# Smaller TensorE prices in a kernel's ordering layer

## The chip, the cores and the metric

The kernel runs on one core of a Trainium2 chip. The metric is the device time of one execution, in microseconds (us). Before the change three runs gave 1128.09, 1132.45 and 1138.17 us, median 1132.45.

## The reference

One inference step of a two-layer backbone for 128 context tokens and 256 latent tokens, model width 1024, all in float32. In a layer:

```
h   = LN(x) * (1 + scale_a) + shift_a            # shift, scale, gate = silu(cond) @ ada_w + ada_b
z   = h @ w_in                                   # 1024 x 2048, split in q, k, v, conv and gating parts
A   = attention(rms(q), rms(k), v)               # 8 q heads, 2 kv heads; latents also see 128 cached keys
B   = c_b * conv3(c_c * c_in)                    # depthwise, width 3
C   = u * (W_s LN(v) + b)                        # over chunks of 128 positions
x   = LN1(alpha * x + gate_a * concat(A, B, C) @ w_out)
h   = LN(x) * (1 + scale_f) + shift_f
x   = LN2(alpha * x + gate_f * FFN(h))
```

FFN is a dense SwiGLU of width 2816 in layer 0 and top-2 of 8 SwiGLU experts of width 1408 in layer 1. There the router's logits choose two experts for each token, and the weights of all eight are read. The outputs are both token streams and each layer's context keys and values.

## The kernel before, in words

**Tiles.** The 384 tokens are three tiles of 128 rows. A product that must keep float32 accuracy takes three matmuls in the fp32r type (`mm3`, L647): both operands are split into a high and a low part. Weights arrive in 1 MB loads into five `st` buffers (768 or 512 KB at the edges of a matrix); ScalarE casts the high part of half a load (`wh`), VectorE subtracts to get the low part (`wl`) (`split`, L630, and `split2`, L1144). 1 MB of weights in a full block of 128 rows feeds 12 matmuls of 512 columns. The modulation (`ada_group`, L731), the small block of 32 rows and the two half blocks of 64 rows (`pair`, L1552) use the raw float32 weights.

**Stages.** Modulation for layer 0, the mixers of layer 0 (`mixers`, L958: `w_in`, attention, convolution, gating, `w_out`), the dense FFN (L1101), the mixers of layer 1, routing (`route`, L1205: LN, transposes, router logits, ranks and lists for three tiles), then the experts (`moe`, L1706): a first full block with a fixed expert, four full blocks in the order of their loads, and a last full block that shares its weights with a small block of 32 rows. The two least loaded experts share one block in two halves of 64 rows. Its 18 steps are put between steps of the full blocks, evenly over the list from the place in `PLACES = (4, 7, 56)` on; this is the shared block in small steps. `scatter` (L1656) and `back` (L1647) add the expert rows to the tokens, and `close_main` (L1675) writes the result.

**The ordering layer.** `Net` calls no engine directly. Each operation goes to `Plan.record` (L285), which notes its operands and gives it a price in ns for each engine that may do it (`price`, L364). `flush` (L403) then plays the program through with one clock for each engine: an operation is ready when those it needs have ended, plus a latency from `LAT` (L349). Of the ready ones of an engine, `flush` takes one that starts within `SLACKS` (50 ns on PE, 60 on DVE) of the time when the engine is free, in the order in which they were recorded, and otherwise the one that starts first. Then the instructions are issued in the order found. Each engine works its list in that order, whatever the real times turn out to be. An operation recorded through `nc.any` may go to one of two engines, and `finish` (L522) picks the one that the planned clocks favour.

A load's price is its bytes at 375 bytes per ns, 2796 ns for 1 MB. Buffers are given out by `find` (L173): a tile may be placed ahead of earlier tiles of its tag only if places are left for all of those. `WINDOW` (380) limits how far the plan looks ahead.

**Filling matmuls.** Where the plan sees PE idle, `keep_warm` (L502) issues matmuls of the identity, whose result nobody reads. They are in the program, and are executed there whether PE is really idle or not. Their number is

```
WARM = (500, 430)
n = int((at - f - WARM[0]) / WARM[1])
```

with `f` the planned time at which PE is free and `at` the planned start of its next operation. A planned gap must so be at least 930 ns to get one, and each further 430 ns gives one more. They are issued at L515; all other planned instructions are issued at L498, or at L500 if they are the second or later matmul of a group.

**Prices of PE before (L376 to L386).** A transpose costs 62 ns if its operand is fp32r, else 109. The 32-row strips of raw float32 cost 0.4167 ns for each column plus 12. The 64-row halves of 512 columns cost half of 1.6667 ns for each column plus 1. An fp32r matmul costs 0.4453 ns for each column plus 4, and at least 112: this is 232 ns for 512 columns and 175 for 384. Other float32 matmuls cost 1.6667 (or 0.85 at half the rows) for each column plus 6, and at least 214.

Of the kernel before, what the change touches and what calls it, by code (L numbers as in the profile page):

```python
# [11 lines left out]
F32R = mybir.dt.float32r  # L12
# [235 lines left out]
class Plan:  # L248
# [115 lines left out]
    def price(self, eng, name, outs, ins, a, k):  # L364

        if name == "call":
            return 1000.0 if outs else 100.0
        if name == "dma_start" and eng != "SP":
            return 60.0
        if eng == "SP":  # L370
            v = outs[0] if outs else ins[0]
            return v.free() * v.cells.shape[0] * 4 * 32 / 375.0
        o = outs[0]
        n = o.free()
        ps_in = any(v.tile.psum for v in ins)
        if eng == "PE":  # L376
            if name == "transpose":
                return 62 if ins[0].dt == F32R else 109
            if o.cells.shape[0] == 1 and ins[0].dt != F32R:
                return n * 0.4167 + 12  # L380
            if o.cells.shape[0] == 2 and len(ins) > 1 and ins[1].dt == F32 and "tile_position" in k and n == 512:
                return n * 1.6667 * o.cells.shape[0] / 4 + 1
            if ins[0].dt == F32R:
                return max(112, n * 0.4453 + 4)
            half = o.cells.shape[0] == 2 or ins[0].cells.shape[0] == 2
            return max(214 if len(ins)>1 else 107, n * (0.85 if half else 1.6667) + 6)  # L386
        if eng == "ACT":
            c = 0.833 * max(n, max([v.free() for v in ins], default=0)) + (55 if ps_in else 90)
            return c + 93 * sum(isinstance(k.get(q), View) for q in ("bias", "scale", "accum_out"))
        if eng == "POOL":  # L390
            if k.get("op") == ALU.pow:
                return 160 * n + 300
            return 2.25 * n + (245 if name == "tensor_scalar" else 80)
        m = max([n] + [v.free() for v in ins])
        if name in ("tensor_copy", "tensor_scalar", "tensor_scalar_add", "tensor_scalar_mul", "tensor_single_scalar"):
            extra = 50 * sum(isinstance(v, View) for v in a[2:])
            return (1.04 if ps_in else 0.52) * m + 70 + extra
        if name == "memset":
            return 0.3 * m + 60
        return 1.04 * m + 70 + (60 if name == "scalar_tensor_tensor" and isinstance(a[2], View) else 0)  # L400
# [1644 lines left out]
```

## Time and profile before

| | |
|---|---|
| median of three runs | 1132.45 us (1128.09 to 1138.17) |
| the profiled execution | 1130.28 us |
| its span, first to last instruction | 1128.5 us |
| mean granted TensorE clock | 0.984 of full |
| PE busy | 1083.0 us (96%), 5256 matmuls |
| DVE busy | 737.1 us (65%) |
| ACT busy | 537.7 us (48%) |
| POOL busy | 123.8 us (11%) |
| moved by DMA | 282.11 MB, mean 250 GB/s |

PE is TensorE's matrix part, PEld its weight loads, DVE VectorE, ACT ScalarE, POOL GpSimd, SP SyncE, which issues the loads. Busy time of PE is the union of its matmuls' intervals, which overlap; the rate of a stream of matmuls is therefore read from starts, not from the duration of one. A float32 matmul that is not fp32r stands in the trace as two matmuls. A waiting time names the engine that ended it. "Issue" is a wait that the profile can't put down to anything.

### The profile page before, as it was taken

The numbers are of one execution on the slowest core, as the hardware profiler recorded it, in microseconds if no ns is written. First come the engines' busy times: TensorE is split into PE (matmuls) and PEld (weight loads), VectorE is DVE, ScalarE is ACT, GpSimd is POOL, SyncE is SP. The second block draws the span as 40 slices with busy tenths as digits, with TensorE's granted clock in tenths as the row PEclk, the third lists the DMA queues.
The fourth block names the chain that finished last, engine by engine and source line by source line (L and its number), as shares of the span: only waits on it lengthen the run. The fifth ranks groups of instructions, "written<-read, shape, count | busy, mean of one in ns | idle before, by whom it ended". The sixth has DMA issues, their size and how long they took to land. (4 is left out here: it accounts for less than half of the span.)

```text
span 1128.5 us, 14587 instructions
## 1 busy us (share of the span) xinstructions
PE 1083.0 (96%) x5256; PEld 771.3 (68%) x5256; DVE 737.1 (65%) x1296; ACT 537.7 (48%) x900; POOL 123.8 (11%) x141
## 2 busy tenths in 40 slices
PE   7999999999999999989999989999999999999995
PEld 4566568877777778857666777666767677676673
DVE  3475769543434444697657896856757677787965
ACT  3544556431323233254554336455656555576652
POOL 3440103100000000034100120000000000002201
PEclk8999999999999999999999979999999999999998
DMA  9877553564647474554367536899889999897541
GB/s 369 311 276 287 193 188 139 197 211 162 238 172 272 150 288 139 222 221 157 118 246 241 204 125 224 321 359 381 332 340 373 389 386 357 341 360 265 212 175 59
DMA packets 49295, 282.11 MB, mean 250 GB/s; under 512 B 6320, under 2 KB 8112, under 8 KB 21312
## 3 DMA queue, kind: packets, MB, share of 16 engines
q1 hardware_dynamic: 47104, 275.51, 64.8%
q0 software_dynamic: 1248, 4.02, 1.0%
q10 hardware_dynamic: 864, 1.57, 0.4%
q8 instruction: 43, 0.70, 0.3%
q14 instruction: 36, 0.29, 0.1%
HBM read 277.63 MB, written 3.46 MB: 249 GB/s over the span
## 5 line engine op out<-in xcount | busy, mean ns | idle before, releaser
L498 PE MATMUL bank<-q,q 128*128 128x512 f32 (+6 forms) x3679 | 875.8, 391 | 4.2 <-DVE q L498 2.4
L498 PEld LDWEIGHTS bank<-q,q 128*128 128x128 f32 (+2 forms) x3679 | 654.5, 189 | 203.9 <-issue 34.4
L498 DVE TENSOR_TENSOR q<-st,q 128x1024 fp32r<-128x1024 f32 (+1 forms) x324 | 373.7, 1184 | 118.6 <-ACT q L498 94.3
L498 ACT CAST q<-st 128x1024 fp32r<-128x1024 f32 (+1 forms) x324 | 318.7, 1018 | 231.0 <-PE bank L498 124.6
L498 DVE TENSOR_TENSOR q<-q,bank 128x512 f32<-128x512 f32 (+3 forms) x121 | 70.5, 592 | 114.9 <-PE bank L498 108.2
L498 ACT COPY q<-bank 128x128 f32<-128x128 f32 (+2 forms) x201 | 64.1, 370 | 88.6 <-PE bank L498 61.3
L498 PE MATMUL bank<-idf,q 128*128 128x128 f32 (+1 forms) x503 | 82.3, 287 | 24.1 <-ACT q L498 10.5
L498 PEld LDWEIGHTS bank<-idf,q 128*128 128x128 f32 (+1 forms) x503 | 59.4, 145 | 63.5 <-ACT q L498 18.8
L498 POOL TENSOR_TENSOR q<-q,nhalf 128x1 f32<-128x1 f32 (+3 forms) x42 | 41.5, 995 | 461.3 <-DVE q L498 461.3
L498 POOL TENSOR_TENSOR q<-q,q 128x512 fp32r<-128x512 f32 (+4 forms) x70 | 66.9, 972 | 220.7 <-ACT q L498 140.9
L498 ACT CAST q<-bank 128x512 fp32r<-128x512 f32 (+2 forms) x58 | 31.7, 554 | 110.4 <-PE bank L498 105.0
L498 PE MATMUL bank<-st,q 128*64 128x512 f32 (+3 forms) x280 | 84.1, 578 | 0.0
L498 DVE TENSOR_TENSOR q<-bank,q 128x512 fp32r<-128x512 f32 (+5 forms) x83 | 50.4, 616 | 44.5 <-ACT q L498 38.9
L500 PE MATMUL bank<-st,q 128*64 128x512 f32 (+1 forms) x140 | 64.2, 581 | 0.0
L498 DVE TENSOR_TENSOR q<-q,q 128x512 f32<-128x512 f32 (+13 forms) x135 | 54.5, 426 | 13.6 <-POOL q L498 10.7
L498 ACT ACTIVATE q<-bank 128x512 f32<-128x512 f32 (+4 forms) x51 | 26.2, 514 | 66.3 <-PE bank L498 57.9
L498 PE MATMUL bank<-st,cs 128*32 128x512 f32 x96 | 47.5, 609 | 1.1 <-DMA st<-in_ada_w_dram 0.8
L500 PE MATMUL bank<-st,cs 128*32 128x512 f32 x288 | 47.9, 609 | 0.0
L498 ACT ACTIVATE q<-bank,q 128x384 f32<-128x384 f32 (+2 forms) x58 | 30.9, 537 | 29.3 <-DVE q L498 22.8
L276 POOL DMA_INDIRECT q<-dr,q x8 | 9.4, 1169 | 313.9 <-DVE q L498 309.8
L498 PEld LDWEIGHTS bank<-st,q 128*64 128x64 f32 (+1 forms) x280 | 20.2, 122 | 33.9 <-issue 33.4
L498 DVE SCALAR_TENSOR_TENSOR q<-q,q,q 128x512 f32<-128x512 f32 (+2 forms) x45 | 41.0, 966 | 0.1
(87 smaller groups left out, 443.2 us busy)
## 6 DMA issues: line engine op xcount, KB each, us to landing
st<-in_ada_w_dram SPq DMA_DIRECT2D x48, 1024.0 KB
st<-in_moe_w2a_dram SPq DMA_DIRECT2D x40, 1024.0 KB
st<-in_moe_w1a_dram SPq DMA_DIRECT2D x32, 1024.0 KB
st<-in_moe_w3a_dram SPq DMA_DIRECT2D x32, 1024.0 KB
st<-in_ffn_w_dram SPq DMA_DIRECT2D x22, 1024.0 KB
st<-in_w_in_dram SPq DMA_DIRECT2D x16, 1024.0 KB
st<-in_moe_w1b_dram SPq DMA_DIRECT2D x16, 768.0 KB
st<-in_moe_w3b_dram SPq DMA_DIRECT2D x16, 768.0 KB
```

Of the source, the lines that this page charges most:

```text
L276: self.nc.gpsimd.indirect_dma_start(out=out, out_offset=None, in_=src.rearrange("p t d -> (p t) d"), in_offset=o)
L498: getattr(self.real[o.eng], o.name)(*a, **k)
L500: getattr(self.real[o.eng], o.name)(*[x.real() if isinstance(x, View) else x for x in b], **q)
```

## The change

Five constants of `price` for PE are replaced. Nothing else in the program is changed: not the operations, not the record order, not the places of the shared block's steps.

```
         if eng == "PE":
             if name == "transpose":
-                return 62 if ins[0].dt == F32R else 109
+                return 57 if ins[0].dt == F32R else 107
             if o.cells.shape[0] == 1 and ins[0].dt != F32R:
-                return n * 0.4167 + 12
+                return n * 0.4167 + 8
             if o.cells.shape[0] == 2 and len(ins) > 1 and ins[1].dt == F32 and "tile_position" in k and n == 512:
                 return n * 1.6667 * o.cells.shape[0] / 4 + 1
             if ins[0].dt == F32R:
-                return max(112, n * 0.4453 + 4)
+                return max(54, n * 0.4167 + 1 if n >= 256 else n * 1.6667 + 1)
             half = o.cells.shape[0] == 2 or ins[0].cells.shape[0] == 2
-            return max(214 if len(ins)>1 else 107, n * (0.85 if half else 1.6667) + 6)
+            return max(107, n * (0.85 if half else 1.6667) + 3)
```

So an fp32r matmul of 512 columns goes from 232 to 214 ns in the plan, one of 384 from 175 to 161, one of a few columns from 112 to 54; a router matmul (8 columns) and a small block's sum (32 columns) from 214 to 107; a transpose from 109 to 107.

## Rows read from the trace of the kernel before

**Rows 1.** Busy time by stage: window, length, engines' busy us, clock, DMA share, GB/s.

```profile
0.00:30.00 30.00, 23.92 (x110) 13.03 (x110) 10.18 (x30) 11.48 (x21) 9.56 (x24) 0.89 0.93 372
30.00:200.00 170.00, 166.78 (x905) 113.11 (x897) 117.71 (x261) 89.63 (x223) 41.68 (x45) 1.00 0.61 230
200.00:460.00 260.00, 258.97 (x1195) 202.76 (x1195) 113.49 (x138) 81.52 (x101) 2.67 (x3) 1.00 0.58 210
460.00:645.00 185.00, 176.88 (x890) 120.46 (x889) 139.99 (x298) 86.07 (x214) 35.01 (x42) 1.00 0.54 193
645.00:700.00 55.00, 48.56 (x228) 39.54 (x228) 45.12 (x133) 26.31 (x35) 9.68 (x10) 0.84 0.47 164
700.00:1100.00 400.00, 392.37 (x1886) 273.10 (x1886) 294.30 (x411) 235.23 (x296) 19.68 (x14) 1.00 0.85 327
1100.00:1128.00 28.00, 15.53 (x58) 9.26 (x54) 16.31 (x28) 7.46 (x13) 5.55 (x6) 0.84 0.16 59
```

**Rows 2.** Timeline of PE: a run of fp32r matmuls and what follows it.

```profile
639.71 7.37 PE L498 MATMUL bank<-q,q 128*128 128x512 f32 x31
646.91 1.55 PE L515 MATMUL bank<-idr 128*128 128x512 f32 x6
```

**Rows 3.** PE's costliest group, shapes apart: count, busy us, mean ns, idle before.

```profile
L498 PE MATMUL bank<-q,q 128*128 128x512 f32 x3036 | 757.4, 401 | 4.2 <-DVE q L498 2.4 <-ACT q L498 1.3
```

**Rows 4.** The filling matmuls' line: windows 0-30, 30-600, 600-700, 700-1128 us.

```profile
L515 PE MATMUL bank<-idr x29: 387/505/797, 1.7 to 23.9; 128*128 128x512 f32 x29
L515 PE MATMUL bank<-idr x4: 396/436/497, 499.5 to 503.2; 128*128 128x512 f32 x4
L515 PE MATMUL bank<-idr x33: 387/397/774, 646.9 to 675.6; 128*128 128x512 f32 x33
L515 PE MATMUL bank<-idr x2: 397/439/481, 901.3 to 951.0; 128*128 128x512 f32 x2
```

**Rows 5.** Timeline of PE in the routing: logits, filling matmuls, transposes.

```profile
651.55 3.54 PE L498 MATMUL bank<-q,q 128*128 128x8 f32 x16
654.94 2.05 PE L515 MATMUL bank<-idr 128*128 128x512 f32 x4
656.94 1.81 PE L498 MATMUL bank<-idf,q 128*128 128x128 f32 x8
658.73 1.95 PE L498 MATMUL bank<-q,q 128*128 128x8 f32 x16
...
673.43 2.52 PE L515 MATMUL bank<-idr 128*128 128x512 f32 x10
678.12 1.18 PE L498 MATMUL bank<-idf,q 128*128 128x128 f32 x8 [2.17 <-DMA q<-dr,q]
```

**Rows 6.** The page's DMA issues: the experts' loads.

```profile
st<-in_moe_w2a_dram SPq DMA_DIRECT2D x40, 1024.0 KB
st<-in_moe_w1a_dram SPq DMA_DIRECT2D x32, 1024.0 KB
st<-in_moe_w3a_dram SPq DMA_DIRECT2D x32, 1024.0 KB
...
st<-in_moe_w1b_dram SPq DMA_DIRECT2D x16, 768.0 KB
st<-in_moe_w3b_dram SPq DMA_DIRECT2D x16, 768.0 KB
...
st<-in_moe_w2b_dram SPq DMA_DIRECT2D x8, 512.0 KB
```

**Rows 7.** Waits of VectorE, experts' stage: who, for whom, us, times, longest.

```profile
DVE q L498 <- PE bank L498: 37.9, 22, 3.9
```

**Rows 8.** Busy time by stage, the 50 us with the busiest VectorE.

```profile
1000.00:1050.00 50.00, 48.87 (x238) 35.48 (x236) 41.99 (x46) 33.70 (x43) 11.21 (x8) 1.00 0.82 309
```

**Rows 9.** Waits of PE's weight loads for ACT and DVE, 460-645 us.

```profile
PEld bank L498 <- ACT q L498: 9.9, 19, 2.5
PEld bank L498 <- DVE q L498: 5.3, 11, 0.8
```

## The prediction

> **What bounds the kernel now.** I read the busy times by stage first [rows 1]. TensorE is the bound nearly everywhere: 258.97 of 260 us in the dense FFN, 392.37 of 400 in the experts, 176.88 of 185 in the second mixers, 166.78 of 170 in the first. All idle time of PE that a better order could remove is therefore small: 3.2 us in the first mixers, 8.1 in the second, 6.4 in the routing, 7.6 in the experts, 25.3 in all. The start (DMA share 0.93) and the tail after 1100 us, where the last LN runs out, hold the rest, and no price of PE changes what is late there.
>
> Then the rate of PE's main work. In a run of 31 fp32r matmuls, starts lie (646.91 - 639.71) / 31 = 232 ns apart [rows 2]. This is exactly the price before. The new price, 214 ns, is 17.7 ns or 7.6% short, and there are 3036 such matmuls [rows 3]: in the plan PE becomes some 54 us shorter, on the chip nothing does. The change removes no operation. It can act only through three things that the plan decides: the order on each engine, the engine of an `any` operation, and the number of filling matmuls.
>
> The Trainium skill (TensorE: Matmul & The Clock Gate, Back-to-back issue gap) gives N / 2.4 + 2.5 ns between matmuls at full clock, 216 for 512 columns, which is the new price. By that rule the new plan would run in step with the chip and the experts' term below would be nothing instead of 2 us. The trace disagrees, with its 232 ns [rows 2], and the measurement decides.
>
> **Part by part.**
>
> *Dense FFN, 200 to 460 us.* PE has 1.0 us idle in 260 [rows 1], the loads take 0.58 of the DMA's time and DVE less than half. Weights are split ahead, up to the buffers. Whatever the order, PE's sum remains: 0 us. The cover is PE's own saturation; it goes only if DVE's list were reordered so that splits came late, and DVE has 146 us free.
>
> *Filling matmuls.* Before there are 29 in the start, 4 at the change of layers, 33 in the routing, 2 in the experts [rows 4]. Each is a real instruction of some 0.23 us at full clock, as any of 512 columns [rows 2]. A cheaper PE is idle longer in the plan, so their number grows.
>
> In the routing, the logits of a tile are 8 matmuls, priced 1.71 us before and 0.86 after, so the gap before the next tile's transposes grows by 0.86 us: 2 more at 430 ns each, for two such gaps 2 to 4 more. (The gap behind the third tile moves as a whole.) Four of them take 2.05 us between two tiles, 0.5 us each at the low clock, and the transposes follow with no idle time shown [rows 5], so here they lie on the path: up to 4 x 0.5 = 2 us lost. Further on, a run of 10 is followed by 2.17 us of waiting for the gathered rows [rows 5]; there they are hidden. On the other side, the granted clock is 0.84 in this stage [rows 1]: between the levels of 1.2 and 2.4 GHz that is about a third of the 55 us, 18 us, at the lower one. If more filling kept a third of these 18 us at the upper level, 6 us of PE's work would take 3 (an estimate). Bounds -3 to +2; I take +1, since the rows show the price and only allow the gain.
>
> In the experts the prices decide what the plan believes to be the bound. Expert loads come to 40 + 32 + 32 of 1 MB, 32 of 768 KB and 8 of 512 KB, or 132 MB [rows 6], 16.5 for each of 8 experts, 46.1 us each at the plan's 2.796. A full block has 162 matmuls of 512 columns and 48 of 384: 46.0 us before, 42.4 after. So far balanced, now bound by loads. The shared block adds a fifth of its 33 MB, 18.5 us, to each of the first five blocks, and a fifth of its 54 groups at 0.856 us and 16 at 0.664, 11.4 us, to PE; transposes and scattering about 4 more. Per block, loads 64.6 us against PE 61.4 before and 57.8 after: planned idle time 3.2 us before, 6.8 after, over five blocks 16 and 34. The 16 us gave 2 filling matmuls [rows 4], since a plain load leaves only 2.80 - 2.57 = 0.22 us and the rule needs 0.93. In proportion 34 give some 4; if all idle time lay in gaps of 0.93, 37. I take 8 more, because a step of the shared block, two loads for 3.4 us of PE, leaves larger gaps: 8 x 0.232 = +2 us. Bounds 0 and 35 x 0.232 = +8.
>
> *Order in mixers and experts.* Two effects of opposite sign. A plan with a short PE puts more matmuls between an operation and the one that waits for its result on another engine: 7.6% more work under each latency, so real operands come earlier than PE needs them. The weight loads now wait 9.9 us for ACT and 5.3 for DVE in the second mixers [rows 9], much of it under running matmuls, so at best half of the 25.3 us idle, some 13, comes back. Against that, attention's chain of softmax, transposes and copies gets its turns later, and DVE and ACT are given operations that wait for PE too early. The constants around it were not changed, and nothing in the trace favours one side. I take 0, bounds -13 and +21 (below).
>
> *The sum.* 1130.28 (span 1128.5 and 1.8 around it) + 0 + 1 + 2 + 0 = 1133.3. The profiled execution lies 2.2 us below the median of the runs, so 1135.5, and I round to **1136 us**, 0.3% slower.
>
> **The rivals.**
>
> *Faster: the plan gains slack.* PE stalls less, because its operands are priced late. All of half the idle time, -13, or a little more with a clock dip spared, -16, gives 1116 to 1120. For it: PE is the bound, and PE waiting is what the plan cannot see now. Against it: the FFN and the experts, 660 us, have 8.6 us idle to give.
>
> *Slower: VectorE's list is set for a PE that is too fast.* In the experts DVE reads PE's sums for the gate and for the scatter, and splits the low weights in the same list. A load's 12 matmuls end 12 x 17.7 = 212 ns later than planned, so DVE stands at a sum that is not there, and the next split stands behind it. For the 99 MB of the six full blocks this is 99 x 0.212 = 21 us if each shows on PE: 1130.3 + 3 + 21 = 1154; with half of it 1144. DVE waits for PE there 22 times already, 37.9 us [rows 7]. Against it: DVE has 106 us free over the stage [rows 1] and six pairs of buffers. It decides where DVE has little room left: at 42.0 busy of 50 [rows 8] 8 us is all the slack there is, and if other 50 us stretches reach that, the waits show. The Trainium skill (TensorE: Matmul & The Clock Gate, Architectural detail) says that VectorE's and ScalarE's queues are strictly first in, first out, which is what this rival needs; no row shows an overtaking.
>
> *Nothing moves.* Tiles get buffers in record order unless places are left over, so lists may come out nearly as before: 1132 us.
>
> **How the numbers follow.** About 1% is what a measurement of this kernel tells from no change. Forecast 0.42, with its own range 1128 to 1144 (the fillers' bounds and some of the order's). Nothing moves 0.13. So 0.55 within 1%. DVE's list 0.30, slower by over 1%; of its terms the fillers' upper bound counts too. Slack 0.15, faster. The range leaves out the far half of the faster case and the last part of the slower one: 1119 to 1154.
>
> **What would show it.** Right: starts of fp32r matmuls still 232 ns apart; the filling line at 72 to 85 instead of 68, two or more added between the routing's tiles; the FFN's 260 us unchanged; PE idle in mixers and experts within some 5 us of now. The slower rival: DVE's wait for PE well above 37.9 us in the experts, and PE busy below 97% there. The faster one: PE's idle time in the second mixers at half of 8.1 us. Wrong would be a change of more than 3 us in the FFN, or a number of filling matmuls above 110, or operations moved between DVE, ACT and POOL by the dozen.

## The result

The changed kernel takes 1139.83 us (median of 20 runs), the kernel before 1130.77 in 20 runs beside it. The ratio is 1.008, with a 95% interval of 1.0066 to 1.0094: slower by 0.8%, or 9 us. The forecast was 1136 us, 0.3% slower. The direction was right and the time lies in the range, but the terms were not: a gain of some 5 to 9 us ahead of the routing, which the sum did not have, was more than lost by two losses that it had far too small.

The page's busy line before and after, then the busy times by stage after, with the windows of [rows 1], the last one longer:

```profile
PE 1083.0 (96%) x5256; PEld 771.3 (68%) x5256; DVE 737.1 (65%) x1296; ACT 537.7 (48%) x900; POOL 123.8 (11%) x141
PE 1088.1 (96%) x5288; PEld 780.4 (69%) x5288; DVE 735.3 (65%) x1294; ACT 535.6 (47%) x904; POOL 118.7 (10%) x139
```

```profile
0.00:30.00 30.00, 23.11 (x112) 11.82 (x113) 10.48 (x30) 12.45 (x23) 10.52 (x24) 0.94 0.93 371
30.00:200.00 170.00, 167.24 (x915) 115.34 (x914) 121.45 (x267) 91.03 (x227) 36.51 (x42) 1.00 0.61 233
200.00:460.00 260.00, 260.00 (x1206) 206.52 (x1206) 114.08 (x137) 82.48 (x102) 3.33 (x2) 1.00 0.58 211
460.00:645.00 185.00, 178.07 (x897) 121.71 (x895) 142.45 (x304) 86.12 (x215) 35.48 (x43) 1.00 0.51 189
645.00:700.00 55.00, 49.05 (x218) 41.81 (x219) 39.69 (x123) 20.92 (x28) 8.41 (x9) 0.75 0.46 161
700.00:1100.00 400.00, 387.01 (x1837) 268.26 (x1839) 288.04 (x405) 233.63 (x298) 18.95 (x14) 1.00 0.85 328
1100.00:1136.00 36.00, 23.61 (x115) 14.98 (x107) 19.07 (x32) 9.00 (x15) 5.55 (x6) 0.89 0.13 46
```

The reader sees PE doing more matmuls in every window up to 645 us, and 49 fewer in the experts' 400 us. Equal windows only hint at this; the same piece of work has to be found in both traces. Behind the last `w_out` product come the filling matmuls, so their start marks its end: 646.91 us before [rows 2], 637.79 after. PE's timeline after, from there to the first expert, and the end:

```profile
637.79 5.62 PE L515 MATMUL bank<-idr 128*128 128x512 f32 x24
648.53 1.97 PE L498 MATMUL bank<-idf,q 128*128 128x128 f32 x8 [5.13 <-ACT q L498]
650.43 1.88 PE L498 MATMUL bank<-q,q 128*128 128x8 f32 x8
652.16 0.67 PE L498 MATMUL bank<-idf,q 128*128 128x128 f32 x2
652.62 1.71 PE L498 MATMUL bank<-q,q 128*128 128x8 f32 x8
654.19 2.37 PE L498 MATMUL bank<-idf,q 128*128 128x128 f32 x10
656.36 4.28 PE L498 MATMUL bank<-q,q 128*128 128x8 f32 x20
660.49 1.09 PE L498 MATMUL bank<-idf,q 128*128 128x128 f32 x4
661.37 2.76 PE L498 MATMUL bank<-q,q 128*128 128x8 f32 x12
663.99 6.46 PE L515 MATMUL bank<-idr 128*128 128x512 f32 x21
...
681.62 11.43 PE L498 MATMUL bank<-q,q 128*128 128x512 f32 x48
...
1122.33 1.28 PE L498 MATMUL bank<-q,q 128*128 128x512 f32 x4
```

The same places before:

```profile
650.22 1.36 PE L498 MATMUL bank<-idf,q 128*128 128x128 f32 x8 [1.75 <-ACT q L498]
...
679.59 12.64 PE L498 MATMUL bank<-q,q 128*128 128x512 f32 x48
...
1114.26 1.28 PE L498 MATMUL bank<-q,q 128*128 128x512 f32 x4
```

Three differences: 9.1 us ahead at the end of `w_out`; 2.0 behind at the first expert, so the routing and the way into it lost 11.2; 8.1 behind at PE's last matmuls, so the experts lost another 6.0. This is one profile of each kernel. Over all profiles, with those of the experiments below, the ten kernels with the new price of the main stream up to the routing end `w_out` at 637.8 to 641.7 us and the four with the old ones at 646.8 to 649.2, so the gain is 7.4 us in the mean, and the pair shown lies above it. Two of the kernels below with the same lists in the experts differ there by 2.8 us, so 6.0 is no sharp number either. PE's nominal work is the same but for 32 more filling matmuls, 100 instead of 68. Their line after, by the places where most were added:

```profile
L515 PE MATMUL bank<-idr x24: 388/389/397, 637.8 to 643.0; 128*128 128x512 f32 x24
...
L515 PE MATMUL bank<-idr x7: 388/397/580, 757.2 to 919.0; 128*128 128x512 f32 x7
```

32 x 0.23 us is 7 us and would by itself pass for the cause. The 5.13 us of waiting behind the 24 speak against it: PE had nothing to do there anyway.

### The profile page after: what moved, and what is told of

It is laid out like the page before. It is cut to its first block, busy times and chain, and to the rows that moved or that the text cites. A ratio compares the mean times of both kernels' runs of the same rounds, so it can differ in the third digit from the quotient of the medians.

```text
span 1136.6 us, 14640 instructions
## 1 busy us (share of the span) xinstructions
PE 1088.1 (96%) x5288; PEld 780.4 (69%) x5288; DVE 735.3 (65%) x1294; ACT 535.6 (47%) x904; POOL 118.7 (10%) x139
## 5 line engine op out<-in xcount | busy, mean ns | idle before, releaser
L498 PE MATMUL bank<-q,q 128*128 128x512 f32 (+5 forms) x3679 | 876.3, 391 | 5.7 <-DVE q L498 3.8
L498 PEld LDWEIGHTS bank<-q,q 128*128 128x128 f32 (+2 forms) x3679 | 655.9, 189 | 202.0 <-issue 35.1
L498 DVE TENSOR_TENSOR q<-st,q 128x1024 fp32r<-128x1024 f32 (+1 forms) x324 | 372.9, 1186 | 102.5 <-ACT q L498 79.4
L498 ACT CAST q<-st 128x1024 fp32r<-128x1024 f32 (+1 forms) x324 | 316.2, 1018 | 188.4 <-PE bank L498 108.1
L498 DVE TENSOR_TENSOR q<-q,bank 128x512 f32<-128x512 f32 (+3 forms) x121 | 70.7, 593 | 128.7 <-PE bank L498 117.7
L498 PE MATMUL bank<-idf,q 128*128 128x128 f32 (+1 forms) x503 | 82.6, 286 | 24.9 <-ACT q L498 10.9
L498 ACT COPY q<-bank 128x128 f32<-128x128 f32 (+2 forms) x201 | 62.3, 364 | 91.3 <-PE bank L498 65.9
L498 ACT CAST q<-bank 128x512 fp32r<-128x512 f32 (+2 forms) x62 | 33.8, 553 | 151.1 <-PE bank L498 140.7
L498 PEld LDWEIGHTS bank<-idf,q 128*128 128x128 f32 (+1 forms) x503 | 61.8, 147 | 61.0 <-DVE q L498 16.9
L498 POOL TENSOR_TENSOR q<-q,q 128x512 fp32r<-128x512 f32 (+5 forms) x68 | 65.9, 985 | 218.0 <-ACT q L498 133.4
L498 DVE TENSOR_TENSOR q<-bank,q 128x512 fp32r<-128x512 f32 (+5 forms) x83 | 50.4, 617 | 57.5 <-ACT q L498 44.2
L498 POOL TENSOR_TENSOR q<-q,nhalf 128x1 f32<-128x1 f32 (+3 forms) x42 | 38.9, 928 | 465.3 <-DVE q L498 463.7
L498 PE MATMUL bank<-st,q 128*64 128x512 f32 (+3 forms) x280 | 86.6, 578 | 0.0
L500 PE MATMUL bank<-st,q 128*64 128x512 f32 (+1 forms) x140 | 63.7, 580 | 0.0
L498 DVE TENSOR_TENSOR q<-q,q 128x512 f32<-128x512 f32 (+13 forms) x137 | 52.8, 408 | 14.8 <-POOL q L498 8.4
L498 ACT ACTIVATE q<-bank 128x512 f32<-128x512 f32 (+4 forms) x51 | 26.3, 515 | 70.4 <-PE bank L498 64.4
L498 PE MATMUL bank<-st,cs 128*32 128x512 f32 x96 | 47.5, 609 | 0.9 <-DMA st<-in_ada_w_dram 0.8
L500 PE MATMUL bank<-st,cs 128*32 128x512 f32 x288 | 47.9, 609 | 0.0
L498 ACT ACTIVATE q<-bank,q 128x384 f32<-128x384 f32 (+2 forms) x58 | 31.0, 540 | 32.3 <-DVE q L498 25.3
L498 PEld LDWEIGHTS bank<-st,q 128*64 128x64 f32 (+1 forms) x280 | 20.8, 122 | 36.6 <-issue 36.1
L498 DVE TENSOR_REDUCE q<-bank 128x1 f32<-128x384 f32 (+6 forms) x64 | 24.3, 412 | 26.5 <-PE bank L500 23.4
```

Source lines behind the costliest of these rows:

```text
L498: getattr(self.real[o.eng], o.name)(*a, **k)
L500: getattr(self.real[o.eng], o.name)(*[x.real() if isinstance(x, View) else x for x in b], **q)
```

## The experiments

Three theories to begin with: **A**, the added filling matmuls are the loss; **B**, the order of the lists is, with a gain ahead of the routing and losses in routing and experts; **C**, one cause ahead of the routing is carried on. All ratios are to the kernel before, run on the same chip.

**As many filling matmuls as before.** Order untouched.

```
+        n = {12: 6, 13: 12, 17: 0, 18: 0, 19: 0, 20: 0}.get(self.places, n)
+        self.places += 1
...
-                order.append(emit)
+                if n:
+                    order.append(emit)
```

> The changed kernel, its order untouched, with the filling matmuls cut from 100 to 68, the number before: 6 instead of 24 ahead of the routing, 12 instead of 21 behind the logits, and 2 instead of 7 in the experts. Theory A (the 32 extra filling matmuls are the loss, 32 x 0.23 = 7 us on PE's path): ratio to before 1.000 to 1.002. Theory B (most of them run while PE waits anyway, since 5.1 us of waiting follow the 24; the loss is in the order of the lists): at most the 5 in the experts and a few in the routing come back, 1 to 3 us, ratio 1.005 to 1.008.

Measured: 1.0073 (1.0052 to 1.0093). A falls. PE's timeline in this kernel shows what took the fillers' place, a wait of 9.21 us for the same ACT operation (an edit moves the line numbers, so L498 is L499 here and in some of the kernels below, and L500 is L501):

```profile
640.22 1.54 PE L518 MATMUL bank<-idr 128*128 128x512 f32 x6
650.96 1.97 PE L499 MATMUL bank<-idf,q 128*128 128x128 f32 x8 [9.21 <-ACT q L499]
```

**New prices up to the routing, old ones from there; and the mirror of it.** `price` got both versions, and `moe` switches.

```
+        if eng == "PE" and not self.late:
...
     def moe(self, l, mid):
+        nc.late = True
```

> New prices for everything recorded before routing, the old ones for routing and experts. Theory B, by the two traces: the stages up to the end of the last w_out gain 9 us, the join to the routing gives them back, the experts, planned with old prices, keep their old speed: 1130 to 1134 us, ratio 0.998 to 1.003. If the gain ahead of the routing really costs the experts time by the way in which they start (theory C: one cause, carried on), ratio 1.006 to 1.010 as with the full change. Theory A goes by the count of filling matmuls, which is some 30 above before up to the first expert and like before in the experts: about +6 us, ratio 1.005.

> The mirror: old prices up to routing, new ones for routing and experts. Theory B: the stages up to the last w_out end as before (about 647 us), the experts lose what they lost with the full change, 6 to 8 us: ratio 1.005 to 1.008. Theory C: no loss in the experts, ratio 0.999 to 1.002. Theory A: the number of filling matmuls is within a few of before, ratio 1.000.

Measured: 0.9968 (0.9945 to 0.9991) and 1.0039 (1.0018 to 1.006). The new prices are worth keeping ahead of the routing and cost time behind it, as B has it; C falls by the first kernel, for which it asked 1.006 or more. Neither ratio lies in B's ranges, though their intervals reach into them: the first kernel is faster than B allows, and the second loses less. In its profile the experts take 436.3 us from first to last matmul, only 1.6 more than before, where 6 to 8 were expected. The parts do not add up (-0.3% and +0.4% against +0.8%): what the join costs depends on the plan on both sides of it. In the first kernel PE's first expert products start at 679.25 us, as before, so the join gives back its whole gain; it wins in the experts, whose prices are the old ones. This last bit, some 5 us in one pair of profiles, may be an order that came out better or in part the spread of profiles; no run here says which.

**Only the fp32r line.**

```
-                return max(112, n * 0.4453 + 4)
+                return max(54, n * 0.4167 + 1 if n >= 256 else n * 1.6667 + 1)
```

> Of the five constants only the fp32r line is changed (232 to 214 ns for 512 columns); transposes, strips and the small float32 matmuls keep their old prices. If the main stream of fp32r matmuls carries both the gain ahead of the routing and the loss in the experts (theory B with the 54 us of plan that this line takes): ratio 1.005 to 1.010, with the end of the last w_out near 638 us. If the loss is from the router's and the small block's halved prices: ratio 0.992 to 1.000.

Measured: 1.0093 (1.0071 to 1.0115). The main stream's price alone does all of it; the router's halved prices, on which a term of the prediction rested, are not needed.

**What in the experts?** Two candidates. B1: PE's price against that of a load makes the plan believe that loads are the bound. B2: the gather's planned delay, which did not shrink, puts its transposes at a bad place.

```
-            return v.free() * v.cells.shape[0] * 4 * 32 / 375.0
+            return v.free() * v.cells.shape[0] * 4 * 32 / (406.0 if self.late else 375.0)
...
+        nc.late = True
```

> The changed kernel with loads recorded from the routing on priced at 406 instead of 375 bytes per ns, so that 1 MB costs 2583 ns: in the plan, loads and PE's 12 matmuls (2572) stand as they stood before the change. Theory B1 (the experts lose because the plan takes them to be bound by loads): the 6 to 8 us lost in the experts come back, ratio to before 1.000 to 1.003. Theory B2 (they lose because PE's transposes of gathered rows are placed too early, since the gather's planned delay of 5 us did not shrink with PE's prices): no change, ratio 1.006 to 1.010, and PE still waits 8 us or more for gathered rows.

```
-            return 4000
+            return 6000
```

> The changed kernel with the planned delay behind a gather raised from 4000 to 6000 ns; the trace shows 6.4 to 7.1 us from issue to landing. Theory B2: PE's waits for gathered rows in the experts (8.7 us on PE, 3.4 before the change) fall below 4 us, and 4 to 7 us come back, ratio 1.002 to 1.005. Theory B1: the waits fall, but the time goes to other waits, ratio 1.006 to 1.009.

Measured: 0.9967 (0.9945 to 0.9988) with cheaper loads, 1.008 (1.0052 to 1.0107) with the longer gather. B1 stands: with PE's prices all small and the old ratio restored behind the routing, the loss is gone, and the kernel is 1.1% faster than the one with PE's prices alone changed. That is more than B1 asked for, because the cheaper loads helped in two places: from first to last matmul the experts take 433.3 us (before 434.7, changed kernel 440.7), and the way from the end of `w_out` to the first expert takes 36.9 us (before 32.7, changed kernel 43.8). That the plan takes loads for the bound is worked out from its prices; no run shows its clocks. B2 falls, though its waits did what was expected. PE's waits for gathered rows, experts' stage, first the changed kernel, then the one with the longer gather:

```profile
PE bank L498 <- DMA q<-dr,q: 8.7, 5, 2.6
```

```profile
PE bank L498 <- DMA q<-dr,q: 2.8, 2, 2.0
```

6 us of waiting went, and no time came back: they were a place where the delay showed, not its cause. PE's waits for VectorE rose from 4.3 to 8.6 us instead.

**The old prices of PE, with dearer and with cheaper loads behind the routing.** The kernel before, 346 or 406 in place of 375.

```
-            return v.free() * v.cells.shape[0] * 4 * 32 / 375.0
+            return v.free() * v.cells.shape[0] * 4 * 32 / (346.0 if self.late else 375.0)
...
+        nc.late = True
```

> The kernel before, with its old prices of PE, but loads recorded from the routing on priced at 346 instead of 375 bytes per ns (3030 ns for 1 MB, 8% more). In the plan the experts are then bound by loads as with the small PE prices, though PE's prices are the measured ones. Theory B1 (the ratio of the two prices decides): the experts lose 4 to 8 us, ratio to before 1.004 to 1.008, and ACT waits for PE longer than the 93 us of before. If PE's prices as such did it (a list set for a PE too fast, without regard to the loads): ratio 0.998 to 1.002.

> The kernel before with loads from the routing on at 406 bytes per ns: in the plan the experts are bound by PE by a wider margin. Theory B1 with a gain beyond the old ratio: loads and casts move further ahead, ratio 0.994 to 0.998. If the old ratio is already on the safe side: 0.999 to 1.001.

Measured: 1.0133 (1.0105 to 1.0162) and 1.0002 (0.998 to 1.0025). No price of PE is changed here, and the loss is there, larger than expected: 10.9 us in the experts and 2.9 on the way into them. A ratio past the old one gains nothing in all: in its profile the experts are 5.6 us quicker, but the first expert starts 2.9 us later.

**What does ACT wait for?** Waits in the experts, 700 to 1100 us (engine, for whom: us, times, longest). Before:

```profile
ACT q L498 <- PE bank L498: 93.3, 61, 6.7
...
ACT q L498 <- DMA st<-in_moe_w1b_dram: 22.6, 6, 7.3
ACT q L498 <- DMA st<-in_moe_w1a_dram: 17.6, 9, 5.9
```

```profile
SPq L498 <- PE bank L500: 73.7, 16, 7.9
```

The changed kernel:

```profile
ACT q L498 <- PE bank L498: 125.0, 55, 8.1
...
ACT q L498 <- DMA st<-in_moe_w1b_dram: 13.5, 4, 5.8
...
ACT q L498 <- DMA st<-in_moe_w1a_dram: 7.3, 4, 5.9
```

```profile
SPq L498 <- PE bank L500: 103.6, 18, 9.0
```

ACT stands 32 us longer at PE's results, and 19 us less at these two loads (29 less at all loads of the experts): the weights lie ready and are not cast. The issue of further loads waits 30 us longer for the shared block's PE steps, which hold `st` buffers, and 14 us less for other PE results (44.3 to 30.3). One place where ACT stands in the changed kernel, in order of time:

```profile
916.91 0.58 ACT L498 CAST q<-bank 128x512 fp32r<-128x512 f32 x1 [8.08 <-PE bank L498]
917.39 1.05 ACT L498 CAST q<-st 128x1024 fp32r<-128x1024 f32 x1
...
918.76 4.84 ACT L498 CAST q<-st 128x1024 fp32r<-128x1024 f32 x5
```

ACT stood 8 us at the cast of a PE result and then did six weight casts, none of which waited for a load. The Trainium skill (TensorE: Matmul & The Clock Gate, Architectural detail) says that ScalarE's queue is strictly first in, first out; these rows agree, since the casts run only after the result's.

The waits for PE of ACT in the kernels that tell B1 apart, in this order: small PE prices with loads at 406 (0.9967), old ones with loads at 346 (1.0133), old ones with loads at 406 (1.0002):

```profile
ACT q L499 <- PE bank L499: 99.0, 59, 7.9
```

```profile
ACT q L499 <- PE bank L499: 128.9, 64, 7.5
```

```profile
ACT q L499 <- PE bank L499: 74.8, 57, 6.1
```

They follow the ratio of the two prices, not PE's price, and so do all profiles here. In the seven kernels whose ratio from the routing on is the old one or on its safe side, ACT waits 68 to 99 us for PE and the experts take 429.1 to 434.7 us; in the six where PE is too cheap against a load, 119 to 130 us and 436.3 to 445.5 us. VectorE's waits for PE do not part the two groups: they are 49.8 us in the changed kernel and 52.6 in the one with cheaper loads, whose experts are quick.

To try the wait itself, the changed kernel got more planned delay behind PE's results, from the routing on:

```
-        return self.LAT[d.eng][o.eng]
+        return self.LAT[d.eng][o.eng] + (1000 if d.eng == "PE" and o.eng != "PE" and d.n >= self.late else 0)
```

> The changed kernel with 1000 ns more planned delay from a PE result to any other engine, from the routing on, so that ACT and DVE place what reads PE's sums behind casts and splits that are ready. If the loss in the experts is ACT standing at a PE result while loaded weights wait for their cast (125 us of ACT's waits for PE after the change, 93 before), most of it comes back: those waits fall below 105 us, ratio to before 1.000 to 1.004. If the delay only makes the plan's chains longer: 1.008 to 1.015.

Measured: 1.0021 (1.0 to 1.0043), and

```profile
ACT q L499 <- PE bank L499: 86.1, 58, 8.4
```

Most of the loss comes back with prices as in the changed kernel. In the profile the experts take 429.2 us, and what is left lies ahead of them: the way from `w_out` to the first expert still takes 43.4 us. The issue of loads waits even longer for the shared block's steps here (110.7 us), so that wait is not what costs the time. The delay holds for VectorE's readers too; that ACT's matter is read from the waits, and no run delays ACT's alone.

**The join, and versions that might beat both.** New prices up to the routing, with 44 filling matmuls ahead of it; with the longer gather; with cheaper loads.

```
+        n = {12: 44}.get(self.places, n)
+        self.places += 1
...
+        nc.late = True
```

> The kernel with new prices up to the routing and old ones from there, with 44 instead of 24 filling matmuls ahead of the routing, its order otherwise untouched. If the routing suffers from the clock, which is at half speed from 652 us on after PE's idle stretch: the fillers cover the stretch up to the first transposes, the logits run at the full clock, and 3 to 5 us are gained against the same kernel with 24, ratio to before 0.992 to 0.994. If VectorE sets the pace there: 0.996 to 0.998. If fillers only cost: 20 x 0.23 = up to 4.6 us lost, ratio 1.000.

> The kernel with new prices up to the routing and old ones from there, with the planned delay behind a gather at 6000 ns. There PE waits 2.5 us for gathered rows, so by theory B2 little is to be had: 0 to 2 us, ratio to before 0.994 to 0.997. By B1 nothing: 0.997. Its order changes with the delay, so a shift of 2 us either way would say nothing of either.

> Small PE prices up to the routing, old ones from there, and loads from there at 406 bytes per ns: both gains together. If they add: ratio to before 0.990 to 0.994. If the second one is the same as keeping the old ratio: 0.996.

Measured: 0.9956 (0.9932 to 0.998), 0.9954 (0.9932 to 0.9976) and 0.9985 (0.9967 to 1.0003). The two gains do not add: the third kernel is not ahead of those with one of them alone. The first two lie within each other's interval and that of 0.9968, so the best of these versions is 0.3 to 0.5% ahead of the kernel before, and which is best is open. The fillers did not bring the clock that they were for. Windows around the routing's logits, granted clock in the third column from the end, with 24 fillers and then with 44:

```profile
637.00:652.00 15.00, 9.88 (x44) 7.87 (x43) 14.55 (x33) 5.40 (x6) 3.06 (x5) 0.92 0.00 1
652.00:664.00 12.00, 12.00 (x72) 11.67 (x71) 9.88 (x21) 5.43 (x9) 1.78 (x2) 0.64 0.50 175
```

```profile
637.00:652.00 15.00, 14.20 (x67) 11.17 (x65) 14.55 (x36) 5.55 (x7) 4.08 (x5) 1.00 0.00 1
652.00:664.00 12.00, 12.00 (x66) 11.71 (x66) 9.09 (x18) 4.00 (x7) 0.67 (x2) 0.58 0.66 219
```

What the join loses can be read from VectorE's list. Its group of four below closes the LN of the third tile; ACT's normalisation is what the first transposes wait for. Before, the normalisation comes ahead of the third tile:

```profile
649.35 1.52 ACT L498 ACTIVATE q<-q,q,q 128x512 f32<-128x512 f32 x2 [1.19 <-DVE q L498]
652.23 3.74 DVE L498 SCALAR_TENSOR_TENSOR q<-q,q,q 128x512 f32<-128x512 f32 x4
```

In the changed kernel it comes behind it:

```profile
643.52 2.73 DVE L498 SCALAR_TENSOR_TENSOR q<-q,q,q 128x512 f32<-128x512 f32 x4
647.67 1.52 ACT L498 ACTIVATE q<-q,q,q 128x512 f32<-128x512 f32 x2 [8.63 <-DVE q L498]
```

From the end of `w_out` to the first transposes the kernel before takes 3.3 us; all eight kernels with the new prices up to the routing and loads at 375 take 10.7, as much longer as the mean gain ahead of it. In the two with loads at 406 the old sequence is back, and they take 3.6:

```profile
643.94 1.52 ACT L499 ACTIVATE q<-q,q,q 128x512 f32<-128x512 f32 x2 [1.50 <-DVE q L499]
646.81 3.77 DVE L499 SCALAR_TENSOR_TENSOR q<-q,q,q 128x512 f32<-128x512 f32 x4
```

## Why the prediction was right, and where it was not

*That nothing on the chip gets shorter, and that the change acts through order and fillers alone*: right. The fp32r line is enough, and the ratio moves both ways with prices only. (The new price is 214 ns; the 216 that the prediction calls the same differs by 2, and nothing hangs on it.) Operations moved between engines by a handful, not by the dozen (VectorE 1296 to 1294, ACT 900 to 904, POOL 141 to 139).

*Dense FFN, 0 us*: a little off. In the window from 200 to 460 us, 1206 matmuls ran after and 1195 before [rows 1]; lined up by the matmuls done, fillers left out, the changed kernel is 4.2 us ahead at 215 us and 6.0 at 460, so 1.8 us were gained there. Busy time shows 1.0 us of idle time at most, so a stage with PE busy in 99.6% of its time still held small stalls that busy time does not show.

*Filling matmuls, +3 us*: the number was too low, 100 against 72 to 85, because the gap ahead of the routing was not in the working; the price was too high. The two or more that were to come between the routing's tiles did not come: the four that stood there [rows 5] went. Cutting the count to 68 moved the ratio by 0.0007, less than the intervals can tell from nothing. A filler costs nothing where PE waits in earnest, and most of the new ones do stand there.

*Order in mixers and experts, 0 us as a balance of two effects*: this is the step that failed. Neither effect is small. What the slack rival (0.15) foretold is there ahead of the routing: the end of `w_out` came 9.1 us earlier in this pair of profiles and 7.4 in the mean, and the kernel that keeps it and returns to the old prices is 0.3% faster than before. The prediction put "at best half of the idle" at 13 us for the whole kernel; 7 to 9 came, from less than the whole. That slack is what brought them is not shown: PE's waits for VectorE and ScalarE in the second mixers fell from 7.8 to 5.0 us, which is less than the gain, and no run tries the latencies.

*Routing, +1 us*: 11.2 with the way into it. Of these, 7.4 go by ahead of the first transposes: ACT's normalisation for the first tile, which the 24 fillers and the 5.13 us wait for, comes after VectorE has finished the LN of all three tiles. The working asked what the routing's own gaps would do, and not whether VectorE's list would let PE use an earlier end of `w_out`. Cheaper loads put the sequence back and 7.1 of the 7.4 us with it, though no run changes that sequence alone. Another 2.6 us lie between the last logits and the ranks, where VectorE does four weight splits in place of two. The low clock adds nothing that shows: from the first transposes to the fillers behind the logits it is 15.5 us after and 15.4 before.

*The slower rival*: right in its mechanism and its place, the experts, but not in its engine. By the waits it is ACT, not VectorE, whose list is set for results that come too early: ACT's waits for PE rose by 32 us, VectorE's by 8.5 (37.9 in [rows 7] and 3.4 for grouped matmuls, to 42.2 and 7.6), and VectorE's stayed high where the loss was gone. The sign that PE would be busy below 97% came true, at 387.01 of 400 us. Its price, up to 21 us, was over three times the 6 us measured. And its reason was incomplete: it took the cause to be PE's lag of 212 ns for each load, while the runs show the ratio of PE's price to a load's: with cheaper loads the lag is still there and the experts lose nothing, and with PE's right prices and dearer loads they lose 10.9 us. The working had this ratio, 46.0 against 46.1 us a block before and 42.4 after, and used it only to count fillers.

So 1136 came out near 1139.83 because the forecast's +3 stands for -9, +11 and +6, of which the 32 fillers are next to no part. That the change acts through the plan alone was right; that the time lies in the range is in good part luck, since three terms of 6 to 11 us, all taken as about nothing, offset one another to 8.

## What to carry to other kernels

In this ordering layer prices matter as ratios between the engines that could be the bound: where two are within a few per cent, a change of one of them can flip what the plan takes for the bound, and with it which work is put first. Under-pricing the bound helped ahead of the routing and hurt where a stream of loads has to be prepared ahead, because readers of its results are then placed in front of that preparation. Why it helped ahead of the routing was not tried further. And a gain counts only if the engine that comes next can use it: here VectorE's list gave the whole of it back. In the trace, look at what the engine that prepares stands at: here a wait for loads was harmless, and a wait for the bound engine's results while loads lie ready went with the loss.

## What the runs showed of the hardware

PE's granted clock in the routing is low while the profile has PE busy throughout: 0.58 in 652 to 664 us of the kernel with 44 fillers, between its two levels of 1.2 and 2.4 GHz, with PE busy 12.00 of 12 us in transposes and matmuls of 8 columns, right after a stretch at 1.00 with fillers. What brought it down is open. An indirect gather took 6.1 to 9.1 us from issue to landing in the experts of the changed kernel, median 7.1, against a plan of 5; pricing it at 7 was worth nothing that shows.
